# A decoder layer with 32 experts on one core: four experts instead of two in the first block, nine blocks instead of ten, and a branch two blocks later

## The chip, the core and the metric

The kernel runs on one core of a Trainium2 chip. The metric is the device time of one execution in microseconds. The kernel before took 979.65 us as the median of 3 runs (979.22 to 981.88). In the traces PE is TensorE (the matrix engine), PEld its weight loads, DVE is VectorE, ACT is ScalarE, and SP is the engine whose queue starts nearly all transfers from device memory (HBM) into the on-chip memory (SBUF). PSUM is the memory that TensorE writes its products into.

## The reference

One layer of a decoder on 256 tokens of width 2048, all in float32: an input projection, eight attention heads beside a convolution module, an output projection and a layer norm. Then comes the part that the change is about, a mixture of 32 experts:

```python
g_top = jnp.argmax(g_logits, axis=-1)              # one of 4 groups
top_p, top_i = lax.top_k(e_prob, EXPERT_TOP_K)     # 2 of the 8 experts in it
combine = (one_hot(expert_ids, N_EXPERTS) * weights[..., None]).sum(1)
h = jnp.einsum('td,edf->tef', t, w_gu)             # w_gu: 32 x 2048 x 512
act = silu(h[..., :256]) * h[..., 256:] * combine[..., None]
out = jnp.einsum('tef,efd->td', act, w_down)       # w_down: 32 x 256 x 2048
```

A second layer norm and a gated embedding (one more 2048 x 2048 product) end the layer. Each token goes to 2 of the 32 experts, so an expert has 16 tokens on average. With the inputs that the reference draws, experts 0 to 3 get 18, 2, 12 and 9 tokens; the counts of the others, in falling order, begin with 46, 43, 37, 31, 29, 29, 25.

## The kernel before

**Weights.** Each expert's weights are 6 loads of 1 MB: four pieces of `gu` (the up product, one per quarter of the 2048 inputs) and two of `dn` (the down product, one per half of the 2048 outputs). All 32 experts are read whatever the routing: 192 loads.

**Blocks.** The experts are worked off in blocks of 128 rows. A block (first rank, places) holds 2 experts with 64 places each or 4 with 32. `gather_steps` picks the tokens of a block by one-hot products (tile `xp`, line 776) and turns them into `XT` (lines 781 and 783). `block` then does the up products (`up`, tile `pg`, line 837), sums the partial results (`fold`, line 845, and `nat`, line 866), applies the activation (line 646), does the down products in two halves (`dp`, line 898), and scatters the result back into `z` (`so`, lines 910, 911 and 913). The products use TensorE in column strips: with 32 places four products stand side by side in the array, with 64 places two. The gather of the next block is woven in between the up products of the current one.

**Ranks.** The order of the experts is found at run time: `selection` sorts them by their token counts and writes the list to `order`; SP reads an expert's number from it (line 632) and loads that expert's weights. `STATIC` experts are put last in this order whatever their counts, so that they are known beforehand. They make up block 0, whose loads (`earlygu`, `earlydn`) need no routing:

```python
STATIC = 2
BLOCKS = ((30, 64), (6, 32), (10, 32), (0, 64), (14, 32), (2, 64), (18, 32), (4, 64), (22, 32), (26, 32))
early = [(("gu", e, g), gu[e, g]) for g in range(4) for e in range(STATIC)]
early += [(("dn", e, k), dn[e, k]) for k in range(2) for e in range(STATIC)]
```

**Slots.** The loads go into a ring of 1 MB slots: `ring2` (6), `ringp` (7) and later `ring3` (2), in the order that `places` yields. A load waits until its slot's last user is done, and SP's queue is worked off in order. At most 8 loads are under way, since each waits for one of eight transfer semaphores. The two `ring3` slots first hold the rows `ln0` and `ln1` that `first_affine` (lines 621 and 622 on DVE) reads, 16 steps in all. `prefetch(n)` emits the next n of the `early` loads.

**The branch.** If an expert has more tokens than places, extra blocks of 128 places would be needed. `spilled` counts such cases on DVE (line 1057), and `spill` (line 1073) branches over code for every possible case, ahead of the block numbered `SPILL_BEFORE`. Every engine takes part in this branch, SP too. The gather of the block behind it isn't woven in anywhere; it stands alone behind the branch.

**Order.** The stretch from the first norm through block 0 is written out by hand: within `in_order` PE, ACT and DVE keep the order of the code, with `next(b0)`, `next(gs0)` and `next(sel)` advancing the block, its gather and the selection. `warm(n, ...)` puts n products without use on TensorE (`W1` behind the router's products, `W2` behind the count). In the last block `embedding` adds products with `pw` (line 1095).

Of the kernel before, what the change touches and what calls it, by code (L numbers as in the profile page):

```python
# [27 lines left out]
NE = 32  # L28
# [8 lines left out]
RING = 7  # L37
# [1 line left out]
RING3 = 2  # L39


STATIC = 2

BLOCKS = ((30, 64), (6, 32), (10, 32), (0, 64), (14, 32), (2, 64), (18, 32), (4, 64), (22, 32), (26, 32))

CAPS = [64] * 6 + [32] * 24 + [64] * 2
SPILL = [(r, n) for r, c in enumerate(CAPS) for n in range(c, min(2 * 128, 2 * 256 // (r + 1) if r < 30 else 256), 128)]
SPILL_BEFORE = 5
W1 = 7
W2 = 4  # L50
WOUT = ((0, (0, 1)), (1, (0, 1)), (2, (0, 1)), (0, (2, 3)), (1, (2, 3)), (2, (2, 3)), (3, (0, 1, 2, 3)))
TAPS = 1.6
STEPS = 2.0
# [20 lines left out]
def _constants():  # L74
    cols, where = [], {}

    def put(name, a):
        full = np.zeros((P, a.shape[1]), np.float32)
        full[: a.shape[0]] = a
        where[name] = (sum(c.shape[1] for c in cols), a.shape[1])  # L80
        cols.append(full)
# [13 lines left out]
    put("kneg", np.full((P, NE), -NE))  # L95
    last = (STATIC - e).clip(0) * np.float32(1e5)
    put("kdiff", (e + last)[:, None] - (e + last)[None])
# [28 lines left out]
def tile_trunk(ctx, tc, xT, x, smalls, consts, win_m, win_v, wout, lnrows,  # L126
# [43 lines left out]
    def load(src, name, into=None):  # L170
        t = into or next(places_[0], ringp).tile([P, D], F32, tag="ring", name=name)
        nc.sync.dma_start(t, src)
        return t
# [28 lines left out]
    @contextmanager  # L202
    def in_order():
        traced = nc.cur_bb.bb.instructions
        mark = traced[-1]
        yield
        start = next(k for k in reversed(range(len(traced))) if traced[k] is mark) + 1
        prev = {}
        for i in traced[start:]:
            if i.engine in (PE.engine, ACT.engine, DVE.engine):  # L210
                if i.engine in prev:
                    tc.add_manual_dep(
                        i, prev[i.engine].name,
                        mybir.DependencyInfo(mybir.DependencyClass.NoSync, mybir.DependencyReason.DATA),
                        reason="in_order")
                prev[i.engine] = i
# [299 lines left out]
    def places():  # L516

        yield from [ring2] * RING2 + [ringp] * RING + [ring2] * RING2
        while True:
            yield from ring3 * RING3  # L520
            yield from [ringp] * RING + [ring2] * RING2

    def prefetch(n):
        for _ in range(n):
            key, src = early.pop(0)
            name = "early{}{}{}".format(*key)
            ready[key] = load(src, name, next(ahead_).tile([P, D], F32, tag="ring", name=name))

    for c, gs in WOUT:
# [20 lines left out]
        if c == 0:  # L550
# [3 lines left out]
            ahead_ = places()  # L554
            early = [(("gu", e, g), gu[e, g]) for g in range(4) for e in range(STATIC)]
            early += [(("dn", e, k), dn[e, k]) for k in range(2) for e in range(STATIC)]
            stock[:] = [2, 1, 1, 1, 1]
# [26 lines left out]
    def norm_stats(sts, pool, name):  # L584
        mv = pool.tile([P, NT, 2], F32, name=f"mv{name}")
        for t in range(NT):
            DVE.bn_aggr(mv[:, t], sts[t])
        r = pool.tile([P, NT], F32, name=f"r{name}")
        tmp = pool.tile([P, NT], F32, name=f"rt{name}")
        rstd_of(mv[:, :, 1], r, tmp, NT)  # L590
        nmr = pool.tile([P, NT], F32, name=f"nmr{name}")
        DVE.scalar_tensor_tensor(nmr, mv[:, :, 0], -1.0, r, op0=ALU.mult, op1=ALU.mult)
        return [(mv[:, t, 0:1], r[:, t:t + 1], nmr[:, t:t + 1]) for t in range(NT)]

    hTh, hTl = [], []

    prefetch(len(early))
    places_[0] = ahead_
    stM.close()
    znp = stH.enter_context(tc.tile_pool(name="znp", bufs=1, side="right"))  # L600
# [386 lines left out]
    with in_order():  # L987
        mvr = norm_stats(st1, bp, "n1")
        warm(W1, "r1")
        sel = selection()  # L990
        gs0 = gather_steps(BLOCKS[0], name(0), by=(pm, comb))
        b0 = block(BLOCKS[0], name(0), static=True)
        aff = first_affine()

        def affine_steps(n):
            for _ in range(n):
                next(aff, None)

        for c in range(NCH):
            first_norm(c)  # L1000
        next(sel)
        warm(W2, "r2")
        next(sel)
        next(gs0)
        next(sel)
        next(gs0)
        next(sel)
        next(gs0)
        next(gs0)
        next(sel)  # L1010
        next(b0)
        affine_steps(3)
        next(gs0)
        next(gs0)
        next(sel)
        next(b0)
        affine_steps(2)
        next(gs0)
        next(gs0)
        ACT.activation(dum, epsc, AF.Silu)  # L1020
        next(sel)
        next(b0)
        affine_steps(3)
        next(gs0)
        next(sel)
        next(gs0)
        next(b0)
        gs1 = gather_steps(BLOCKS[1], name(1))
        next(gs1)
        affine_steps(8)  # L1030
        stB.close()
        stC = ExitStack()
        cp = stC.enter_context(tc.tile_pool(name="cp", bufs=1))
        next(b0)
        for _ in range(2):
            next(gs1)
        next(b0)
        for _ in range(2):
            next(gs1)
        next(b0)  # L1040
        for _ in range(2):
            next(gs1)
        next(b0)
        for _ in range(3):
            next(gs1)
        next(b0)
        b1 = block(BLOCKS[1], name(1))
        for _ in range(4):
            next(b1)
        for _ in b0:  # L1050
            pass

    def spilled():

        over = sp.tile([P, len(SPILL), NT], F32, tag="over", name="over")
        for i, (r, n) in enumerate(SPILL):
            DVE.tensor_scalar(over[:, i], poss[:, :, r], float(n), None, op0=ALU.is_gt)
        many = sp.tile([P, 1 + len(SPILL)], F32, tag="many", name="many")
        DVE.tensor_reduce(many[:, 1:], over, axis=AX.X, op=ALU.add)
        DVE.tensor_reduce(many[:, 0:1], many[:, 1:], axis=AX.X, op=ALU.add)  # L1060
        total = pst([P, CH], "total", "x")
        PE.matmul(total[0:1, :1 + len(SPILL)], C("ones")[:, 0:1], many, start=True, stop=True)
        flags = rp.tile([1, 1 + len(SPILL)], I32, name="flags")
        DVE.tensor_copy(flags, total[0:1, :1 + len(SPILL)])
        return flags
# [33 lines left out]
    flags = spilled()  # L1099
    last = len(BLOCKS) - 1  # L1100
    for i, shape in enumerate(BLOCKS):
        if not i:
            continue
        if i == SPILL_BEFORE:
            spill(flags, any_)
# [5 lines left out]
        if i == last:  # L1111
            stH.close()
            gp_ = ctx.enter_context(tc.tile_pool(name="gp", bufs=1, side="right"))
            side, share, total = embedding(gp_), 5, 16
        if i == SPILL_BEFORE - 1:
            any_ = counted(flags, 0)
        coming = iter(())
        if i < last and i + 1 != SPILL_BEFORE:
            coming = gather_steps(BLOCKS[i + 1], name(i + 1))
# [208 lines left out]
```

## Time and profile before

| | |
|---|---|
| median of 3 runs | 979.65 us (979.22 to 981.88) |
| the profiled execution | 983.18 us, its span 981.3 us |
| busy: PE, PEld, DVE, ACT | 909.4, 596.4, 521.8, 356.4 us |
| moved | 294.48 MB, mean 300 GB/s |
| mean granted TensorE clock | 0.97 |

All rows below come from that one execution, in microseconds from the start of its span. Its own time is 3.5 us above the median. The stretches that matter here: the router and block 0 from 358 to 418.5, blocks 1 to 4 from 418.5 to 602.1, the branch from 602.1 to 614.6 with a gather behind it until 623, blocks 5 to 8 from 623 to 814.4, block 9 (the last) until 876.2, and from there the gate product to the end. A busy PE says little about what bounds the kernel, since PE is busy in stretches of both kinds; what a stretch moves per microsecond says more.

### The profile page before, as it was taken

What the parts mean: (1) busy time and instruction counts of PE and PEld (TensorE: products, weight loads), DVE (VectorE), ACT (ScalarE), POOL (GpSimd) and SP (SyncE); (2) the same over time, 40 slices, a digit from 0 to 9 for tenths busy, and PEclk for the clock granted to TensorE, in tenths of its full rate; (3) what the DMA queues carried; (4) which work ended last, traced back from release to release, by engine and by line L of the source; (5) the groups of instructions that cost most, each with busy time, mean ns of one, the idle gap of its engine ahead of it and who ended that gap; (6) DMA issues with size and microseconds to landing.
All of it is one profiled execution on the core that took longest, in us unless ns stands there. A gap on an engine that the chain in (4) does not pass through costs nothing. (4 is left out here: it accounts for less than half of the span.)

```text
span 981.3 us, 14211 instructions
## 1 busy us (share of the span) xinstructions
PE 909.4 (93%) x5339; PEld 596.4 (61%) x5339; DVE 521.8 (53%) x1110; ACT 356.4 (36%) x698; POOL 3.0 (0%) x14
## 2 busy tenths in 40 slices
PE   7999999999999989998989974999899988989997
PEld 7999889999878875443434311634343432247886
DVE  6989898889887455434141303123222321067875
ACT  6454455666684343212212110211111211226553
POOL 0000000000000000000000000000000000000000
PEclk9999999999999989999999978899999999999999
DMA  9868755445459348699999998988999799995721
GB/s 343 357 166 272 297 199 171 150 162 173 157 192 403 135 158 300 262 404 423 424 424 423 425 423 338 424 349 297 415 424 373 296 425 425 424 419 206 229 73 43
DMA packets 44622, 294.48 MB, mean 300 GB/s; under 512 B 5160, under 2 KB 5800, under 8 KB 10240
## 3 DMA queue, kind: packets, MB, share of 16 engines
q1 hardware_dynamic: 43568, 290.85, 75.5%
q0 software_dynamic: 976, 2.63, 1.7%
q8 instruction: 44, 0.72, 0.3%
q14 instruction: 34, 0.28, 0.1%
HBM read 289.78 MB, written 3.67 MB: 299 GB/s over the span
## 5 line engine op out<-in xcount | busy, mean ns | idle before, releaser
L837 PE MATMUL pgb<-gub,XTb 128*32 128x512 f32 (+1 forms) x960 | 149.0, 607 | 7.1 <-DMA gub<-in_gu_dram 7.0
L776 PEld LDWEIGHTS xpb<-Sb,zn 128*128 128x128 f32 x640 | 80.2, 199 | 59.3 <-issue 41.7
L357 DVE SCALAR_TENSOR_TENSOR yall<-u,sml,yall 128x256 f32<-128x256 f32 x240 | 108.6, 478 | 0.3
L776 PE MATMUL xpb<-Sb,zn 128*128 128x128 f32 x640 | 92.4, 294 | 14.6 <-PEq L1073 12.6
L783 DVE TENSOR_SCALAR XTb<-xpb,gbc 128x128 f32<-128x128 f32 x80 | 32.7, 409 | 124.4 <-ACT XTb L781 121.3
L898 PE MATMUL dpb<-dnb,aTb 128*32 128x512 f32 (+1 forms) x480 | 94.7, 612 | 1.0 <-DVE aTb L877 0.9
L781 ACT ACTIVATE XTb<-xpb,gbc 128x128 f32<-128x128 f32 x80 | 36.6, 458 | 148.2 <-PE xpb L776 148.0
L837 PEld LDWEIGHTS pgb<-gub,XTb 128*32 128x32 f32 (+1 forms) x960 | 36.2, 115 | 79.1 <-issue 57.2
L646 DVE SCALAR_TENSOR_TENSOR atb<-atb,wb,natb 128x256 f32<-128x256 f32 x10 | 4.8, 480 | 118.2 <-ACT atb L645 118.1
L913 DVE TENSOR_TENSOR z<-z,sob 128x512 f32<-128x512 f32 x76 | 49.7, 683 | 31.4 <-PE sob L911 31.3
L177 DVE TENSOR_TENSOR Ylb<-dpb,Yhb 128x512 fp32r<-128x512 f32 x40 | 26.4, 687 | 73.6 <-ACT Yhb L176 73.6
L176 ACT CAST Yhb<-dpb 128x512 fp32r<-128x512 f32 x40 | 22.3, 588 | 113.3 <-PE dpb L898 112.1
L845 ACT COPY pgsb<-pgb 128x512 f32<-128x512 f32 x32 | 18.8, 586 | 94.1 <-PE pgb L837 91.0
L898 PEld LDWEIGHTS dpb<-dnb,aTb 128*32 128x32 f32 (+1 forms) x480 | 22.3, 116 | 46.9 <-issue 40.4
L910 PE MATMUL sob<-Yhb,sctb 128*128 128x512 f32 x76 | 34.9, 487 | 15.0 <-DVE z L913 7.5
L910 PEld LDWEIGHTS sob<-Yhb,sctb 128*128 128x128 f32 x76 | 13.6, 192 | 53.3 <-issue 21.6
L911 PE MATMUL sob<-Ylb,sctb 128*128 128x512 f32 x76 | 30.6, 430 | 0.1
L866 PE MATMUL natb<-pgsb,cst 128*32 128x512 f32 (+1 forms) x64 | 20.7, 616 | 4.9 <-ACT pgsb L845 4.9
L911 PEld LDWEIGHTS sob<-Ylb,sctb 128*128 128x128 f32 x76 | 14.2, 200 | 5.9 <-DVE Ylb L177 5.6
L1095 PE MATMUL pl<-pw,pT 128*128 128x512 f32 x32 | 16.9, 652 | 0.0
L837 PE MATMUL pgb<-earlygu,XTb 128*64 128x512 f32 x64 | 16.3, 657 | 0.0
L866 PEld LDWEIGHTS natb<-pgsb,cst 128*32 128x32 f32 (+1 forms) x64 | 3.9, 116 | 17.5 <-ACT pgsb L845 13.5
(2528 smaller groups left out, 1943.1 us busy)
## 6 DMA issues: line engine op xcount, KB each, us to landing
gub<-in_gu_dram SPq DMA_DIRECT2D x120, 1024.0 KB, 18.4
dnb<-in_dn_dram SPq DMA_DIRECT2D x58, 1024.0 KB, 17.1
wo<-in_wout_dram SPq DMA_DIRECT2D x16, 1024.0 KB, 4.9
wg<-in_wgate_dram SPq DMA_DIRECT2D x16, 1024.0 KB, 5.8
wv<-in_win_v_dram SPq DMA_DIRECT2D x8, 1024.0 KB, 23.5
wk<-in_win_m_dram SPq DMA_DIRECT2D x8, 1024.0 KB, 4.8
wq<-in_win_m_dram SPq DMA_DIRECT2D x8, 1024.0 KB, 4.8
earlygu<-in_gu_dram SPq DMA_DIRECT2D x8, 1024.0 KB, 9.5
```

Of the source, the lines that this page charges most:

```text
L176: ACT.copy(h, src)
L177: return DVE.tensor_tensor(l, src, h.bitcast(F32), op=ALU.subtract)
L357: yield DVE.scalar_tensor_tensor(y, u[:, k:k + T], cw[:, c, k:k + 1], y, op0=ALU.mult, op1=ALU.add)
L776: PE.matmul(xp[:, k], zn[t][:, kt * P:(kt + 1) * P], S[:, t, :P], start=t == 0, stop=t == 1)
L781: ACT.activation(xs[:, 0], xp[:, 0], AF.Identity, bias=gbc[:, 1, kt:kt + 1], scale=gbc[:, 0, kt:kt + 1])
L783: DVE.tensor_scalar(xs[:, 1], xp[:, 1], gbc[:, 0, kt:kt + 1], gbc[:, 1, kt:kt + 1], op0=ALU.mult, op1=ALU.add)
L837: PE.matmul(pgs_[e][j * M:(j + 1) * M], XT[:, k, e * M:(e + 1) * M], gp[k], start=kt < G, stop=kt >= KT - G, tile_position=(0, j * M) if G ...
L866: PE.matmul(nat[e * M:(e + 1) * M], C(st), folds[e], start=True, stop=True, tile_position=(0, e * M))
L898: last = PE.matmul(dps[n][j * M:(j + 1) * M], aT[:, k, e * M:(e + 1) * M], dp[e][2 * k + n % 2], start=k == 0, stop=k == 1, tile_position= ...
L910: PE.matmul(o, table(n)[:, ts_], Yh[n], start=True, stop=False)
L911: PE.matmul(o, table(n)[:, ts_], Yl[n], start=False, stop=True)
L913: DVE.tensor_tensor(zs, zs, o, op=ALU.add)
```

## The change

Block 0 takes four experts with 32 places each. Of the other 28 ranks, four have 64 places and 24 have 32, in eight blocks. The branch stands ahead of block 7. The loads of block 0 become 24; 13 of them are emitted before the first norm, and 4, 4 and 3 behind the first three groups of block 0's up products. `W1` goes from 7 to 14 and `W2` from 4 to 2.

```diff
-STATIC = 2
-BLOCKS = ((30, 64), (6, 32), (10, 32), (0, 64), (14, 32), (2, 64), (18, 32), (4, 64), (22, 32), (26, 32))
-CAPS = [64] * 6 + [32] * 24 + [64] * 2
-SPILL_BEFORE = 5
-W1 = 7
-W2 = 4
+STATIC = 4
+BLOCKS = ((28, 32), (4, 32), (0, 64), (8, 32), (2, 64), (12, 32), (16, 32), (20, 32), (24, 32))
+CAPS = [64] * 4 + [32] * 28
+SPILL_BEFORE = 7
+W1 = 14
+W2 = 2
...
-    prefetch(len(early))
+    prefetch(RING)
...
         next(b0)
+        prefetch(4)
         affine_steps(3)
...
         next(b0)
+        prefetch(4)
         affine_steps(2)
...
         next(b0)
+        prefetch(3)
         affine_steps(3)
```

The list of cases behind the branch grows from 21 to 25 (`SPILL`, whose bound for the known experts now goes by `NE - STATIC`).

On SP's queue, at the end of the output projection and before block 1, this stands in the kernel before (`earlydn10` is the first half of expert 1's down weights, `gub100` the first load of block 1, and the brackets name what a row waits for):

```order
L172 DMA earlydn00_4114<-in_dn_dram 128x2048 [waits DMAHW0_49,DVE_49]
L172 DMA earlydn10_4116<-in_dn_dram 128x2048 [waits DMAHW1_49,DVE_49]
L172 DMA earlydn01_4118<-in_dn_dram 128x2048 [waits DMAHW3_49,DMAHW2_49,DVE_49]
L172 DMA earlydn11_4120<-in_dn_dram 128x2048 [waits DMAHW4_49,DVE_49]
L172 DMA ln0_4131<-in_lnrows_dram 128x2048 [waits PE_49]
L172 DMA ln1_4133<-in_lnrows_dram 128x2048 [waits DMAHW5_49]
L632 TENSOR_LOAD order_4140 [waits DVE_49]
L172 ISA
L172 DMA gub100_4554<-in_gu_dram 128x2048 [waits DMAHW6_49,DVE_49]
```

In the changed kernel the same place, from `ln1` on, reads:

```order
L172 DMA ln1_4135<-in_lnrows_dram 128x2048 [waits DMAHW6_49]
L172 DMA earlygu13_4298<-in_gu_dram 128x2048 [waits DMAHW7_49,PE_49]
L172 DMA earlygu23_4300<-in_gu_dram 128x2048 [waits DMAHW0_49,PE_49]
L172 DMA earlygu33_4302<-in_gu_dram 128x2048 [waits DMAHW1_49,PE_49]
L172 DMA earlydn00_4304<-in_dn_dram 128x2048 [waits DMAHW2_49,PE_49]
L172 DMA earlydn10_4352<-in_dn_dram 128x2048 [waits DMAHW3_49,PE_49]
L172 DMA earlydn20_4354<-in_dn_dram 128x2048 [waits DMAHW4_49,PE_49]
L172 DMA earlydn11_4401<-in_dn_dram 128x2048 [waits DMAHW5_49,PE_49]
L172 DMA earlydn30_4356<-in_dn_dram 128x2048 [waits DMAHW6_49,DVE_49]
L172 DMA earlydn01_4358<-in_dn_dram 128x2048 [waits DMAHW7_49,DVE_49]
L172 DMA earlydn21_4403<-in_dn_dram 128x2048 [waits DMAHW0_49,PE_49]
L172 DMA earlydn31_4405<-in_dn_dram 128x2048 [waits DMAHW1_49,PE_49]
```

Eleven loads of known experts now stand between `ln1` and the reading of `order`; two of them, `earlydn30` and `earlydn01`, take the `ring3` slots and wait for DVE, and everything behind them on SP waits with them.

On PE, at block 0's fourth group of up products, the kernel before has (`srt` and `wpb0` are the end of the selection and of the gather, `xpb10` the gather of block 1):

```order
L748 MATMUL srt_4362<-perm_4143,tsb_4342 128x32 x4
L794 MATMUL wpb0_4371<-cst_72,Swb0_4368 128x1 x2
L837 MATMUL pgb00_4271<-earlygu03_4110,XTb06_4333 64x512 x4
L837 MATMUL pgb01_4276<-earlygu13_4112,XTb06_4333 64x512 x4
L776 MATMUL xpb10_4403<-Sb1_4384,zn0_4126 128x128
```

and the changed kernel:

```order
L748 MATMUL srt_4417<-perm_4145,tsb_4383 128x32 x4
L794 MATMUL wpb0_4428<-cst_72,Swb0_4423 128x1 x2
L837 MATMUL pgb00_4278<-earlygu03_4122,XTb06_4374 32x512 x4
L837 MATMUL pgb01_4283<-earlygu13_4298,XTb06_4374 32x512 x4
L837 MATMUL pgb02_4288<-earlygu23_4300,XTb06_4374 32x512 x4
L837 MATMUL pgb03_4293<-earlygu33_4302,XTb06_4374 32x512 x4
L776 MATMUL xpb10_4472<-Sb1_4449,zn0_4128 128x128
```

The group has four experts of 32 places in place of two of 64; three of its four loads are among the eleven that are emitted late.

## Rows read from the trace of the kernel before

**Rows 1.** Page, part 2: GB/s moved in 40 equal slices of the span.

```profile
GB/s 343 357 166 272 297 199 171 150 162 173 157 192 403 135 158 300 262 404 423 424 424 423 425 423 338 424 349 297 415 424 373 296 425 425 424 419 206 229 73 43
```

**Rows 2.** Windows, start:end, length; busy (x count) per engine; PE clock, DMA share, GB/s.

```profile
369.70:394.00 24.30, 23.72 (x128) 12.16 (x129) 15.07 (x43) 8.22 (x19) 0.00 (x0) 0.93 0.83 303
394.00:418.50 24.50, 22.23 (x120) 12.37 (x116) 10.90 (x43) 7.51 (x16) 0.00 (x0) 0.93 0.74 277
...
467.10:512.40 45.30, 40.48 (x287) 17.13 (x286) 12.26 (x27) 9.34 (x20) 0.00 (x0) 1.00 1.01 424
512.40:557.60 45.20, 42.15 (x189) 18.75 (x188) 11.94 (x23) 7.88 (x17) 0.00 (x0) 1.00 1.01 425
557.60:602.10 44.50, 36.49 (x223) 10.10 (x222) 8.88 (x15) 5.63 (x11) 0.00 (x0) 0.88 0.92 378
602.10:623.00 20.90, 7.95 (x49) 7.67 (x49) 4.21 (x15) 2.29 (x5) 0.00 (x0) 0.67 1.01 419
...
670.20:719.00 48.80, 43.67 (x294) 18.51 (x293) 14.43 (x31) 9.23 (x20) 0.00 (x0) 0.96 0.99 393
...
814.40:876.20 61.80, 56.18 (x266) 16.80 (x266) 10.77 (x18) 13.11 (x24) 0.00 (x0) 0.95 1.02 423
```

**Rows 3.** Windows again, cut where the rate of the transfers changes.

```profile
420.00:580.00 160.00, 145.12 (x906) 58.80 (x894) 41.15 (x82) 29.01 (x61) 0.00 (x0) 0.98 1.01 423
580.00:600.00 20.00, 16.82 (x83) 5.28 (x82) 6.18 (x11) 3.28 (x7) 0.00 (x0) 0.88 0.80 322
640.00:700.00 60.00, 55.26 (x322) 24.24 (x321) 15.96 (x36) 12.60 (x27) 0.00 (x0) 1.00 0.87 338
740.00:780.00 40.00, 37.25 (x188) 17.16 (x190) 13.34 (x29) 8.34 (x18) 0.00 (x0) 1.00 0.81 320
```

**Rows 4.** Page, part 6: issues of `gu` loads, size, median us to landing.

```profile
gub<-in_gu_dram SPq DMA_DIRECT2D x120, 1024.0 KB, 18.4
```

**Rows 5.** Groups by line and form, up products of block 2, then of block 3.

```profile
L837 PE MATMUL pgb<-gub,XTb 128*32 128x512 f32 x128 | 15.5, 595 | 0.0
...
L837 PE MATMUL pgb<-gub,XTb 128*64 128x512 f32 x64 | 15.9, 602 | 0.0
```

**Rows 6.** Timeline of PE in block 0: start, us, instruction, count.

```profile
370.88 3.65 PE L837 MATMUL pgb<-earlygu,XTb 128*64 128x512 f32 x16
...
376.44 3.65 PE L837 MATMUL pgb<-earlygu,XTb 128*64 128x512 f32 x16
...
389.31 5.35 PE L837 MATMUL pgb<-earlygu,XTb 128*64 128x512 f32 x16
...
402.94 3.65 PE L898 MATMUL dpb<-earlydn,aTb 128*64 128x512 f32 x16
```

**Rows 7.** Timeline of DVE, the last two steps of the affine.

```profile
393.27 0.68 DVE L621 SCALAR_TENSOR_TENSOR z<-zn,ln 128x512 f32<-128x512 f32 x1
...
394.01 0.68 DVE L622 SCALAR_TENSOR_TENSOR z<-ln,z 128x512 f32<-128x512 f32 x1
```

**Rows 8.** Timeline of SP's queue: block 1's first loads, and around the branch.

```profile
369.68 50.30 SPq L172 DMA_DIRECT2D gub<-in_gu_dram  x16
...
559.62 16.37 SPq L172 DMA_DIRECT2D dnb<-in_dn_dram  x8
597.10 4.89 SPq L172 DMA_DIRECT2D gub<-in_gu_dram  x8
```

**Rows 9.** Timeline of PE, first instruction behind the branch.

```profile
614.61 5.94 PE L776 MATMUL xpb<-Sb,zn 128*128 128x128 f32 x32 [12.59 <-PEq L1073]
```

**Rows 10.** Timeline of PE around the warming products.

```profile
359.82 1.36 PE L242 MATMUL warmr<-cst 128*128 128x128 f32 x10
363.39 0.21 PE L697 MATMUL pos<-Aas,cbtri 128*128 128x32 bf16 x1 [2.21 <-DVE Aas L694]
...
364.10 2.08 PE L242 MATMUL warmr<-cst 128*128 128x128 f32 x8
```

**Rows 11.** Groups of PE in the last block: busy, mean ns, idle before.

```profile
L837 PE MATMUL pgb<-gub,XTb 128*32 128x512 f32 x128 | 19.0, 631 | 3.7 <-DMA gub<-in_gu_dram 3.6
```

More of the change, by code (lines that the diff above doesn't have):

```diff
@@ L39 @@
 RING3 = 2
-STATIC = 2
-BLOCKS = ((30, 64), (6, 32), (10, 32), (0, 64), (14, 32), (2, 64), (18, 32), (4, 64), (22, 32), (26, 32))
-CAPS = [64] * 6 + [32] * 24 + [64] * 2
-SPILL = [(r, n) for r, c in enumerate(CAPS) for n in range(c, min(2 * 128, 2 * 256 // (r + 1) if r < 30 else 256), 128)]
-SPILL_BEFORE = 5
-W1 = 7
-W2 = 4
+STATIC = 4
+BLOCKS = ((28, 32), (4, 32), (0, 64), (8, 32), (2, 64), (12, 32), (16, 32), (20, 32), (24, 32))
+CAPS = [64] * 4 + [32] * 28
+SPILL = [(r, n) for r, c in enumerate(CAPS) for n in range(c, min(2 * 128, 2 * 256 // (r + 1) if r < NE - STATIC else 256), 128)]
+SPILL_BEFORE = 7
+W1 = 14
+W2 = 2
 WOUT = ((0, (0, 1)), (1, (0, 1)), (2, (0, 1)), (0, (2, 3)), (1, (2, 3)), (2, (2, 3)), (3, (0, 1, 2, 3)))
```

## The prediction

> **What bounds the kernel now.** I read the rate of the transfers over the whole span first, because PE is busy nearly everywhere and so says little. From slice 18 on (24.5 us each, so from 417 us) the row stands at 423 to 425 for long stretches, with dips to 338, 349, 297, 373 and 296 [rows 1]. No stretch stays above that level, so 424 GB/s is what this chip moves when it always has something to move. One load of 1024 KB [rows 4] is 1.0486 MB and takes 1.0486 / 424 = 2.473 us; a block of four experts is 24 loads or 59.4 us, a block of two 12 loads or 29.7 us.
>
> Then I set the blocks beside it. Block 2 (32 places) takes 45.3 us and block 3 (64 places) 45.2 us, both at 424 to 425 GB/s [rows 2]. PE's time is the same for both kinds: the up products are 15.5 us for four experts in four strips and 15.9 us for two in two strips [rows 5]. So on PE a block costs about 45 us whatever its kind, while its weights cost 59.4 or 29.7 us. The expert stage is two chains of nearly equal length that lean on each other through 15 slots. Where blocks with 32 places follow each other, PE ends up waiting for weights: block 4 has 36.5 us of work in 44.5 us and a clock of 0.88 [rows 2], and the last block waits 3.6 us for `gub` [rows 11]. Where blocks with 64 places come, the slots are full and the transfers wait: 640 to 700 moves 338 GB/s, 740 to 780 moves 320 [rows 3]. Before the stage, from 369.7 to 418.5, the transfers run at 303 and 277 GB/s [rows 2], since they wait for slots.
>
> **The change part by part.**
>
> *Blocks.* The bytes stay: 192 loads. One block of two experts, 45.2 us of PE time by [rows 2], goes, and block 0 takes four experts in the time of two, since its up group of 3.65 us [rows 6] becomes 32 instructions in four strips, a fourth of the 128 that took 15.5 us [rows 5], so 3.9 us. Behind it block 0 gets four more instructions of `nat` and four of transposes on PE; at the 0.6 us of one instruction [rows 5] that is under 5 us, and about a fourth of it where four strips run side by side. I cost it at nothing: the transfers set the pace from there on, and if they didn't, it would be some 1 to 2 us. PE loses a whole block; whether the end follows depends on the transfers, so I count these.
>
> *Head start.* Before, 303 x 24.3 + 277 x 24.5 = 14.15 MB or 13.5 loads move between 369.7 and 418.5 [rows 2]; with the 12 loads of block 0 already there that is 25.5 of 192 at the start of block 1. After, 13 are there. The next seven loads (three `earlygu`, four `earlydn`) wait for slots that block 0's first two groups free. The first group runs 370.88 to 374.5, so an expert's quarter is free at about 371.8; the second ends at 380.1 [rows 6]. Seven loads take 17.3 us and are in by about 391. Then SP's queue stands at `earlydn30` until DVE has read `ln0` for the last time, at 393.27 + 0.68 = 394.0, and `ln1` 0.8 us later [rows 7]. From 394.0 on nothing holds it but the rate: 24.5 / 2.473 = 9.9 loads until 418.5. That makes 13 + 7 + 9.9 = 29.9, a lead of 4.4 loads or 10.9 us. Block 0 doesn't suffer: `earlygu13` to `earlygu33` are in by about 382 and are used from 389.3; `earlydn30` by 394 + 5 = 399 and is used from 402.9 [rows 6]. If DVE's affine came later, stream and products would slip with it one for one. The lead is at least 0 (the old rate) and at most 12.
>
> *Dips.* In 640 to 700 the shortfall is 60 x (1 - 338/424) = 12.2 us, in 740 to 780 it is 40 x (1 - 320/424) = 9.8 us [rows 3], together 22.0. After, the slots don't fill. At 45.2 us a block the stream delivers 18.3 loads: a block of two gains 6.3 loads on PE, a block of four loses 5.7. From a lead of some 6 loads at block 1 the order 32, 64, 32, 64, 32, 32 goes to about 2, 8, 2, 8, 3 and then to waiting in block 6. It never reaches 15, so all 22.0 us come back. The least I would allow is half, 11.
>
> *Branch.* SP issues block 4's last load at 576 and the next at 597.1 [rows 8]; 580 to 600 lacks 20 x (1 - 322/424) = 4.8 us [rows 3]. PE stands still 12.59 us [rows 9], and with the lone gather behind the branch 602.1 to 623 is 20.9 us [rows 2]. Ahead of block 7 the same things happen once, with the transfers just as full, so I leave both prices as they are. What PE's sequencer waits for the row doesn't say; between half the price and twice it lie 6 us less and 12 us more, and that stays in the range.
>
> *The end of the stream.* 192 loads and 2.25 for the embedding are wanted. Before: 418.5 + (194.25 - 25.5) x 2.473 + 22.0 + 4.8 = 862.6, and the last block ends at 876.2 [rows 2], 13.6 us later. After: 418.5 + (194.25 - 29.9) x 2.473 + 4.8 = 829.7, and with the same 13.6 us behind it 843.3.
>
> *PE as a check.* Block 6's last load is number 144: 418.5 + 114.1 x 2.473 = 700.7. Block 4's last load, issued at 576 [rows 8], was in by about 593 (17 to 18 us behind the issue [rows 4]), and PE left the block at 602.1 [rows 2], some 10 us later; so now it reaches the branch at 710.7. With 20.9 us for branch and gather, 48.8 us for a block of four like block 6 of before and 61.8 us for the last [rows 2] the end is 842.2. The two chains agree within 1.1 us. They hand over to each other, and after waits PE runs with a lower clock (0.88 in block 4, 0.67 around the branch [rows 2]); I add 2 us and take 845.2, that is 31 us less than 876.2.
>
> On the bandwidth the Trainium skill speaks too. Its page "DMA: Bandwidth & Descriptors", section "Where 436 GB/s comes from", gives a ceiling of 435.2 GB/s for the 16 ports. By that figure a load would take 2.409 us, the stream of the changed kernel would end near 819, and PE's chain of 842 would decide alone. The trace's fullest rows stand at 424 to 425, so I keep these.
>
> *Warming products.* Ten of them took 1.36 us, and PE idled 2.21 us behind them [rows 10]. Fourteen instructions more are about 1.9 us and fit into that gap; four instructions less behind the count save up to 1.0 us of the 2.08 us [rows 10]. A clock kept up there could give another 1.8 us at the start of the gather, and an overrun could cost 1.7. I take 0 of the range -2.8 to +1.7. The four added steps of `spilled` on DVE stand among the affine's: 0.5 us at most, inside the lead's bounds.
>
> *The sum.* Lead 10.9 and dips 22.0 give 32.9 us of stream, less 2 for the handover: 31. The span goes from 981.3 to about 950.3 and the profiled execution from 983.18 to 952.2. That execution lies 3.5 us above the median of the runs, so I set the 31 against the median: 979.65 - 31 = 948.6.
>
> **The rivals.**
>
> *The queue stands longer.* Eleven loads now precede the reading of `order`, and two wait for DVE. If DVE's affine ended not at 394 but behind the next down products, at about 406 [rows 6], or the branch cost 12 us more where the stream is full, the gain would be 31 - 12 = 19: 960.7. For it speaks that SP is strictly in order; against it that the affine stands on DVE ahead of everything that block 0 needs later.
>
> *PE decides alone.* If the transfers had reserves, the whole block would come off: 979.65 - 45.2 = 934.5. Against it: no full slice of [rows 1] exceeds 425.
>
> *The clock falls, and it ends slower.* The place is the blocks of four behind waiting weights. There the row of the block that waited shows a granted clock of 0.88 against 1.00 in those that didn't [rows 2]. Eight blocks have about 7 x 41.3 + 56.2 = 345 us of PE work and 33 us besides; between 420 and 876.2, less the branch's 20.9, lie 435 us. So it turns slower from a mean granted clock of 345 / (435 - 33) = 0.86 on; at 0.82 it is 19 us slower, 998.6. Against it: the last block waited 3.6 us and still has 0.95 [rows 2, 11], and my sum has waits only in block 6 and the last. The Trainium skill holds for it: "TensorE: Matmul & The Clock Gate", section "HAM oscillation — how this bites in real kernels", describes a kernel whose products wait for transfers again and again and start each burst on the low clock. Here that would be the blocks of four.
>
> *It isn't the same work.* With 32 places for experts 0 to 3, one with over 32 tokens would take the branch and add a block of its own, 45 us or more: 994 or above. Their counts are 18, 2, 12 and 9, and rank 4 has 29, so nothing spills.
>
> **How the numbers follow.** The forecast gets 0.82 (its own range 943 to 955: lead and branch a few us either way), the longer queue 0.10, PE alone 0.04, the clock 0.03, spilling 0.01. The range goes to 938 and 961: it leaves out PE alone, the slower cases and the worst of the longer queue. About 0.3%, 3 us, is what a measurement of this kernel can tell from no change. Faster by more: 0.82 + 0.04 + 0.08 of the longer queue = 0.94; within it 0.02; slower 0.04.
>
> **What would show it.** In the changed kernel the transfers run at 424 GB/s from about 394 to 700 without a dip, then one dip at the branch, and on to about 830. SP issues `earlydn30` near 394. Block 0 has 32-place products and starts block 1 within 2 us of 418.5. PE waits for `gub` in block 6, a few us, and in the last block. The last block ends near 845, with the 105 us behind it unchanged. I am wrong if dips remain between 420 and 690, if block 0 stalls for `earlydn`, or if the granted clock of the blocks of four lies under 0.9.

## The result and the profile after

The changed kernel takes 947.77 us as the median of 4 runs (947.23 to 949.38); the kernel before, in 4 runs beside it, takes 979.43 us (978.40 to 981.88). The ratio is 0.9676, with a 95% interval of 0.9654 to 0.9697: 31.7 us faster. The forecast was 948.6 us, 31 us less. The profiled execution of the changed kernel is the one of 947.23 us (span 945.5), so it stands close to its median, while that of the kernel before stands 3.5 us above its own. Two traces set side by side therefore show some 4 us more than the change's 31.7.

First the rate of the transfers over the whole span, the page's row in 40 slices (23.6 us each here), against [rows 1]:

```profile
GB/s 334 368 179 242 325 203 188 140 174 152 160 179 329 264 184 271 332 420 423 424 420 423 422 421 422 421 421 424 421 316 418 420 420 422 417 418 209 217 78 33
```

From the 18th slice on (402 us) the row stands at 417 to 424 until the expert stage ends, with a single dip, 316, at the branch. Before there were five. Next come the stretches of the changed kernel, cut at the blocks (start:end, length; busy and count of PE, PEld, DVE, ACT, POOL; granted clock, DMA share, GB/s): block 0 in two parts, blocks 1, 2, 3 and 6, branch and gather, block 7, the last block, the rest.

```profile
363.50:388.50 25.00, 24.32 (x195) 13.49 (x197) 15.62 (x45) 8.88 (x22) 0.00 (x0) 0.93 0.72 295
388.50:412.00 23.50, 21.11 (x166) 11.95 (x162) 10.97 (x46) 8.28 (x18) 0.00 (x0) 1.00 0.96 392
412.00:472.20 60.20, 49.20 (x301) 19.38 (x300) 16.92 (x36) 9.34 (x20) 0.00 (x0) 0.91 1.01 422
472.20:517.40 45.20, 42.15 (x189) 18.76 (x188) 12.66 (x27) 7.89 (x17) 0.00 (x0) 1.00 1.01 422
517.40:563.30 45.90, 41.09 (x291) 17.66 (x290) 13.14 (x29) 9.24 (x20) 0.00 (x0) 1.00 1.01 421
...
655.00:707.00 52.00, 37.16 (x219) 8.91 (x218) 7.54 (x13) 5.62 (x11) 0.00 (x0) 0.92 0.91 373
707.00:723.50 16.50, 8.79 (x44) 8.01 (x44) 5.22 (x17) 1.83 (x4) 0.00 (x0) 0.69 1.01 420
723.50:774.50 51.00, 46.14 (x318) 20.86 (x316) 12.83 (x26) 11.33 (x25) 0.00 (x0) 1.00 1.01 420
774.50:840.10 65.60, 55.16 (x266) 16.52 (x266) 10.80 (x18) 13.14 (x24) 0.00 (x0) 0.95 1.02 418
840.10:945.50 105.40, 98.89 (x453) 78.96 (x451) 77.19 (x138) 54.63 (x98) 0.00 (x0) 0.99 0.45 164
```

The two kernels can be set against each other on one axis. These windows are of the kernel before; the second set, behind it, is of the changed kernel with the same cuts.

```profile
340.00:363.50 23.50, 20.39 (x107) 16.65 (x106) 15.09 (x47) 10.49 (x18) 0.00 (x0) 0.99 0.50 180
363.50:412.00 48.50, 45.97 (x261) 28.00 (x262) 26.00 (x90) 16.36 (x36) 0.00 (x0) 0.89 0.73 272
412.00:418.50 6.50, 6.18 (x22) 2.20 (x18) 1.74 (x3) 1.17 (x2) 0.00 (x0) 0.83 0.43 147
418.50:840.00 421.50, 371.94 (x2137) 154.59 (x2136) 107.55 (x221) 74.56 (x158) 0.00 (x0) 0.96 0.96 396
```

```profile
340.00:363.50 23.50, 21.95 (x135) 18.57 (x134) 15.11 (x52) 11.33 (x18) 0.00 (x0) 1.00 0.60 219
363.50:412.00 48.50, 45.42 (x357) 25.44 (x359) 26.60 (x90) 17.16 (x39) 0.00 (x0) 0.96 0.84 342
412.00:418.50 6.50, 6.10 (x42) 2.28 (x42) 3.85 (x8) 0.59 (x1) 0.00 (x0) 1.00 1.02 423
418.50:840.00 421.50, 357.33 (x2058) 144.46 (x2057) 100.34 (x207) 74.82 (x157) 0.00 (x0) 0.96 1.00 415
```

Up to 418.5 the first three rows give 180 x 23.5 + 272 x 48.5 + 147 x 6.5 = 18.4 MB before and 24.5 MB after: 6.1 MB or 5.8 loads more, 14.4 us of stream at 424 GB/s. From there to 840 the rate is 415 in place of 396 GB/s: 19 x 421.5 = 8.0 MB, 7.6 loads, 18.9 us. Together that is 33 us of stream. The last block ends at 840.06 in place of 876.2 [rows 2], and what follows it takes 105.4 us, 105.1 before. Of these 36.1 us, 2.6 arise ahead of block 0: the warming products `warmr` behind the router start at 357.22, not 359.82 [rows 10]. The change does nothing there; in the eight traces of kernels that have it this start lies between 357.22 and 360.07, so the 2.6 us are spread among executions.

Where PE waits for weights in the changed kernel, from the view of its waits (line, releaser: us in total, times, longest) and its timeline in block 1, the branch and the last block:

```profile
PE pgb L837 <- DMA gub<-in_gu_dram: 22.1, 15, 6.4
...
PE xpb L776 <- DVE Sb L766: 7.6, 1, 7.6
...
PE dpb L898 <- DMA dnb<-in_dn_dram: 2.6, 2, 2.1
```

```profile
411.94 3.64 PE L837 MATMUL pgb<-gub,XTb 128*32 128x512 f32 x32
...
434.42 1.07 PE L837 MATMUL pgb<-gub,XTb 128*32 128x512 f32 x8 [1.43 <-DMA gub<-in_gu_dram]
436.90 1.06 PE L837 MATMUL pgb<-gub,XTb 128*32 128x512 f32 x8 [0.57 <-DMA gub<-in_gu_dram]
439.38 1.07 PE L837 MATMUL pgb<-gub,XTb 128*32 128x512 f32 x8 [1.42 <-DMA gub<-in_gu_dram]
...
715.94 7.67 PE L776 MATMUL xpb<-Sb,zn 128*128 128x128 f32 x40 [7.60 <-DVE Sb L766]
...
786.22 1.94 PE L837 MATMUL pgb<-gub,XTb 128*32 128x512 f32 x8 [6.36 <-DMA gub<-in_gu_dram]
```

In block 1 PE takes eight products of 1.07 us, then waits up to 1.4 us, so that one load of 2.49 us follows the other: PE follows the stream. The waits stand in blocks 1, 6 and the last, 24.7 us in all.

SP's queue in the changed kernel, the counterpart of [rows 8]:

```profile
366.32 2.04 SPq L172 DMA_DIRECT2D earlygu<-in_gu_dram  x3
368.89 21.82 SPq L172 DMA_DIRECT2D earlydn<-in_dn_dram  x8
391.52 30.81 SPq L172 DMA_DIRECT2D gub<-in_gu_dram  x16
...
664.02 17.72 SPq L172 DMA_DIRECT2D dnb<-in_dn_dram  x8
703.43 30.87 SPq L172 DMA_DIRECT2D gub<-in_gu_dram  x16
```

At the branch SP issues nothing for 703.43 - 681.74 = 21.7 us; before it was 597.1 - 576.0 = 21.1.

### The profile page after: what moved, and what is told of

Read it like the earlier page. It is cut to its first block, busy times and chain, and to the rows that moved or that the text cites. A ratio compares the mean times of both kernels' runs of the same rounds, so it can differ in the third digit from the quotient of the medians.

```text
span 945.5 us, 13989 instructions
## 1 busy us (share of the span) xinstructions
PE 862.3 (91%) x5263; PEld 575.2 (61%) x5263; DVE 509.1 (54%) x1090; ACT 349.5 (37%) x684; POOL 3.0 (0%) x14
## 5 line engine op out<-in xcount | busy, mean ns | idle before, releaser
L837 PE MATMUL pgb<-gub,XTb 128*32 128x512 f32 (+1 forms) x896 | 135.6, 621 | 22.2 <-DMA gub<-in_gu_dram 22.1
L776 PEld LDWEIGHTS xpb<-Sb,zn 128*128 128x128 f32 x576 | 71.7, 199 | 45.7 <-issue 28.7
L776 PE MATMUL xpb<-Sb,zn 128*128 128x128 f32 x576 | 81.7, 292 | 8.4 <-DVE Sb L766 7.6
L837 PEld LDWEIGHTS pgb<-gub,XTb 128*32 128x32 f32 (+1 forms) x896 | 31.6, 115 | 93.2 <-issue 50.6
L898 PE MATMUL dpb<-dnb,aTb 128*32 128x512 f32 (+1 forms) x448 | 82.6, 603 | 3.3 <-DMA dnb<-in_dn_dram 2.6
L177 DVE TENSOR_TENSOR Ylb<-dpb,Yhb 128x512 fp32r<-128x512 f32 x36 | 23.5, 687 | 70.8 <-ACT Yhb L176 70.8
L913 DVE TENSOR_TENSOR z<-z,sob 128x512 f32<-128x512 f32 x68 | 44.5, 684 | 19.3 <-PE sob L911 19.2
L910 PE MATMUL sob<-Yhb,sctb 128*128 128x512 f32 x68 | 29.6, 467 | 17.3 <-DVE z L913 9.3
L911 PE MATMUL sob<-Ylb,sctb 128*128 128x512 f32 x68 | 26.6, 423 | 0.0
L837 PE MATMUL pgb<-earlygu,XTb 128*32 128x512 f32 x128 | 16.5, 651 | 0.0
L1099 ACT COPY ple<-pl 128x512 f32<-128x512 f32 x8 | 4.7, 586 | 28.5 <-PE pl L1098 28.5
## 6 DMA issues: line engine op xcount, KB each, us to landing
wv<-in_win_v_dram SPq DMA_DIRECT2D x8, 1024.0 KB, 23.5
```

The costliest lines, as they stand in the source:

```text
L776: PE.matmul(xp[:, k], zn[t][:, kt * P:(kt + 1) * P], S[:, t, :P], start=t == 0, stop=t == 1)
L837: PE.matmul(pgs_[e][j * M:(j + 1) * M], XT[:, k, e * M:(e + 1) * M], gp[k], start=kt < G, stop=kt >= KT - G, tile_position=(0, j * M) if G ...
L898: last = PE.matmul(dps[n][j * M:(j + 1) * M], aT[:, k, e * M:(e + 1) * M], dp[e][2 * k + n % 2], start=k == 0, stop=k == 1, tile_position= ...
L910: PE.matmul(o, table(n)[:, ts_], Yh[n], start=True, stop=False)
L911: PE.matmul(o, table(n)[:, ts_], Yl[n], start=False, stop=True)
L913: DVE.tensor_tensor(zs, zs, o, op=ALU.add)
```

## The experiments

All times are medians. Ratios are to the kernel before as measured beside each run. The kernel before that stood beside e11 and e12 took 973.62 us in its one run, less than any other run of it, so the times of these two say nothing; only their traces are used.

| run | based on | us | ratio (95%) |
|---|---|---|---|
| the change | | 947.77 | 0.9676 (0.9654 to 0.9697) |
| e3_fewer_bytes | after | 909.46 | 0.9287 (0.9250 to 0.9323) |
| e4_less_pe | after | 947.13 | 0.9677 (0.9649 to 0.9706) |
| e5_no_hold | after | 943.58 | 0.9644 (0.9616 to 0.9672) |
| e6_order | after | 970.79 | 0.9926 (0.9896 to 0.9956) |
| e1_warm_old | after | 952.49 | 0.9723 (0.9700 to 0.9745) |
| e2_branch5 | after | 948.15 | 0.9674 (0.9651 to 0.9696) |
| e7_block0_alone | after | 950.16 | 0.9694 (0.9671 to 0.9718) |
| e8_before_warm | before | 969.02 | 0.9903 (0.9867 to 0.9940) |
| e9_before_w1 | before | 968.30 | 0.9883 (0.9851 to 0.9916) |
| e10_before_w2 | before | 975.22 | 0.9955 (0.9932 to 0.9978) |
| e11_before_w2_1 | before | 975.63, one run | |
| e12_before_w2_3 | before | 980.77, one run | |

**Do the transfers or PE set the end?** The theory is the forecast's: the stream of loads does. The rival is that PE's lost block alone made the gain. One run, e3, takes bytes away (it leaves out the second half of the down weights of blocks 1 to 7), the other, e4, takes away PE's work.

```diff
+                    elif hf and not static and not done:
+                        dp[e] = first_half[e]
...
-                        dp[e] = weights_of("dn", e, hf)
+                        dp[e] = first_half[e] = weights_of("dn", e, hf)
```

> The changed kernel, but in blocks 1 to 7 the second half of each expert's down weights isn't loaded: the products of that half read the first half again, so the result is not the reference's. 24 of the 192 loads go, 24 x 2.488 = 60 us of stream, no product goes. Theory (the stream of weights sets the pace behind block 0): the stream chain drops out, PE's own chain decides, that is seven blocks at 45 to 48 us, the branch, and the last block without its waits: the last block ends near 808 instead of 840, 30 to 34 us earlier, about 915 us. Rival (PE decides alone already): nothing changes, 948 us.

```diff
-PE.matmul(o, table(n)[:, ts_], Yh[n], start=True, stop=False)
-PE.matmul(o, table(n)[:, ts_], Yl[n], start=False, stop=True)
+PE.matmul(o, table(n)[:, ts_], Yh[n], start=True, stop=True)
```

> The changed kernel without the second product of each scatter (the low parts Yl at line 911), except in the closing half of the last block, so the result loses precision. PE loses 8 x 0.42 = 3.4 us in a block, 27 us in all; no load goes. Theory (stream): only what lies behind the last loads counts, 1 to 4 us faster, 944 to 947 us. Rival (PE decides alone): 25 to 27 us faster, about 922 us.

Fewer bytes gave 38 us, less work on PE 0.6 us, inside the interval. PE's busy time fell by 10.3 us (862.3 to 852.0) and not by 27, at a granted clock of 0.94 in place of 0.96 from 418.5 to 840, and even these 10 us don't show in the time. With less work PE only waits longer (its waits in e4_less_pe, against 22.1 and 2.6):

```profile
PE pgb L837 <- DMA gub<-in_gu_dram: 24.6, 20, 7.0
...
PE dpb L898 <- DMA dnb<-in_dn_dram: 3.7, 3, 2.0
```

The 60 us of stream that e3 takes away don't all come back. Its row of the page shows where they stay: the dips return (322, 314, 333, 363, 299), as they stood in the kernel before. PE also stands 13.0 us at the branch in e3, not 7.6.

```profile
GB/s 338 377 173 229 314 225 188 162 166 158 154 172 197 420 144 226 318 341 423 421 423 422 369 424 421 322 314 423 419 333 363 299 423 408 412 421 174 224 65 35
```

**Does the order of the blocks matter, as the slot argument says?** Here all blocks of 32 places but the last come first.

```diff
-BLOCKS = ((28, 32), (4, 32), (0, 64), (8, 32), (2, 64), (12, 32), (16, 32), (20, 32), (24, 32))
+BLOCKS = ((28, 32), (4, 32), (8, 32), (12, 32), (16, 32), (20, 32), (0, 64), (2, 64), (24, 32))
```

> The changed kernel with the blocks in another order: 28 (known), 4, 8, 12, 16, 20 with 32 places, then 0 and 2 with 64, then 24. The same blocks, bytes and products. Theory: blocks of four in a row make PE wait (13.9 us each in blocks 2 to 5), and two blocks of two behind the branch then find the slots full, so the stream idles: some 24 us slower, 965 to 975 us. Rival (the dips of the kernel before came from its two blocks more with 64 places and not from their places in the order): 948 us.

970.79: 23 us of the gain are gone with the same bytes and the same products. The lead is used up early, and PE waits 35.5 us for `gub`. Then the blocks of 64 places fill the slots: the stretch from 770 to 800 moves 114 GB/s, which lacks 30 x (1 - 114/424) = 21.9 us.

```profile
PE pgb L837 <- DMA gub<-in_gu_dram: 35.5, 34, 1.7
```

```profile
770.00:800.00 30.00, 28.44 (x147) 14.01 (x146) 5.68 (x13) 6.70 (x15) 0.00 (x0) 1.00 0.31 114
```

**What does SP's standing at `earlydn30` cost?** The late loads of known experts go to slots that PE frees, none to a `ring3` slot, so that SP doesn't wait for the affine.

```diff
-        yield from [ring2] * RING2 + [ringp] * RING + [ring2] * RING2
+        yield from ([ring2] * RING2 + [ringp] * RING) * 2 + [ring2] * RING2
```

> The changed kernel with another order of slots: the late loads of block 0 take slots of the ring that block 0's first groups free, and the two slots that wait for DVE's affine come into the order only behind them. SP's queue then never stands at earlydn30. Between 363 and 388.5 the stream ran at 295 GB/s of 422, which is 7.5 us short. Theory (stream): 5 to 7 us of this come back and the end moves by as much: 941 to 943 us. Rival (the head start isn't worth its time, since PE's chain is as long): 0 to 2 us, 946 to 948 us.

943.58 (942.77 to 945.12 in 6 runs): 4.2 us less than the change by the medians, 3.1 us by the ratios; no run of one lies among those of the other, though the intervals of the ratios overlap. In its queue block 1's loads begin at 382.02 and not at 391.52, and PE waits 17.3 us for `gub`:

```profile
370.02 11.19 SPq L172 DMA_DIRECT2D earlydn<-in_dn_dram  x8
382.02 37.51 SPq L172 DMA_DIRECT2D gub<-in_gu_dram  x16
```

So the hold is real; its price, 3 to 4 us, lies between the two theories (5 to 7 and 0 to 2) and in neither. This version is the fastest found, 35 us below the kernel before.

**What are the branch's place and the warming products worth?**

```diff
-SPILL_BEFORE = 7
+SPILL_BEFORE = 5
```

> The changed kernel with the branch ahead of block 5 instead of block 7. Theory (stream): SP stands still for about 21 us once wherever the branch is, the stream loses 4 to 6 us once, and PE's standstill is hidden behind waits for weights later: within 2 us of 947.8. Rival (the place of the branch is worth time of its own, since PE's standstill of some 16 to 21 us with the lone gather lands on the chain): 5 us or more in either direction.

```diff
-W1 = 14
-W2 = 2
+W1 = 7
+W2 = 4
```

> The changed kernel with the old numbers of warming products (7 and 4). In the trace of the changed kernel the first gather ran in 3.1 us instead of 4.9 and block 0 began 8.7 us behind the router's second product group instead of 11.9. Theory (the warming products keep the clock up, DVE's affine ends earlier, and the stream with it): 2 to 3.5 us slower, 950 to 951 us. Rival (my forecast's term, 0): within 1 us of 947.8.

e7_block0_alone has both edits, so that only the blocks and the late loads are left of the change.

> The main part alone: four known experts with 32 places in block 0, nine blocks and the late loads, but the old warming products (7 and 4) and the branch ahead of block 5. Theory: all of the gain but the 2 to 3.5 us of the warming products, 950 to 951 us. Rival (the branch's place carries a part): 955 us or more.

The branch's place is worth nothing (0.9674 and 0.9676); SP's gap there is 21.8 us. Without the new warming products the changed kernel is 4.7 us slower, and its interval doesn't meet the change's; between e7 and e2, with the branch ahead of block 5, it is 2.0 us, with intervals that overlap. Blocks and late loads put alone on the kernel before give 29.2 us, against 31.7 for the whole change.

The traces of the kernels with this order of blocks and all the bytes bear out the stream: e1, e2, e4, e5, e7 and the change all move 415 GB/s from 418.5 to 840. They differ in what moves from 340 to 418.5: 288 and 291 GB/s with the old warming products (e7, e1), 298 to 312 with the new (e2, e4, the change), 329 in e5, the fastest.

Then the warming products alone, on the kernel before (`W1 = 14`, `W2 = 2`):

> The kernel before with only the new numbers of warming products (14 and 2). Theory: block 0 begins 3 us earlier there too, and since block 0's known weights are loaded by then and PE is on the chain behind it, the end comes 1 to 3.5 us earlier, 976 to 978.5 us. Rival (it helps only where the stream's start hangs on it): 979.4 within 1 us.

A miss: it is 10.4 us faster, three times the theory's most. PE's timeline shows two causes. In the changed kernel, as in this run, the stretch from the router's warming products to block 0 reads (here of the changed kernel, against [rows 10]):

```profile
357.22 2.92 PE L242 MATMUL warmr<-cst 128*128 128x128 f32 x24
360.79 0.19 PE L697 MATMUL pos<-Aas,cbtri 128*128 128x32 bf16 x1 [0.64 <-DVE Aas L694]
...
361.41 0.71 PE L242 MATMUL warmr<-cst 128*128 128x128 f32 x4
361.96 1.06 PE L776 MATMUL xpb<-Sb,zn 128*128 128x128 f32 x8
363.09 2.08 PE L776 MATMUL xpb<-Sb,zn 128*128 128x128 f32 x16
365.10 3.77 PE L837 MATMUL pgb<-earlygu,XTb 128*32 128x512 f32 x32
```

The 14 added instructions fill the gap and delay nothing: `pos` starts 3.57 us behind the start of `warmr` in both. The gather behind runs on the upper level of the clock, 2.4 GHz (granted clock 1.00 from 357.2 to 365.1; 0.60 from 365.9 to 370.9 before): 8 products in 1.06 us, which took 1.91 before, and 16 in 2.08 against 2.94. From `pos` to the first up product it is 4.3 us in place of 7.5. In e8 block 0 starts 3.1 us earlier as well (367.82). The other cause lies at the branch: PE stands still 6.75 us there and not 12.59. Two questions followed: is it `W1` or `W2`, and why does the standstill change? Two runs change one of the numbers each.

```diff
-W1 = 7
+W1 = 14
```

> The kernel before with W1 = 14 alone (W2 stays at 4): 14 more warming instructions ahead of the count, none taken away behind it. With W1 = 14 and W2 = 2 together the kernel before came to 969.0 instead of 979.4, and PE's standstill at the branch fell from 12.6 us to about 6.8. Theory, the clock through the selection does it: block 0 then starts about 2 us earlier (3 us less about 1 us of products that stay behind the count), the standstill at the branch is about 7 us or 12.6 as may be, and the time is 970 to 974. Rival, the standstill depends on how many instructions lie ahead of the branch on PE: with 14 more instead of 10 more it may be of either size, and the time follows it: about 970 with a short one, about 977 with a long one, block 0 starting 2 us earlier in both.

```diff
-W2 = 4
+W2 = 2
```

> The kernel before with W2 = 2 alone (W1 stays at 7): 4 warming instructions less behind the count. Theory, the clock through the selection does it and W2 only takes away its own time: block 0 starts within 1 us of 370.9, the standstill of PE at the branch stays near 12.6 us, and the time is 977 to 980. Rival, the standstill depends on the place of the branch in PE's instructions: then 4 instructions less could shorten it to about 7 us without any change at the selection, and the time would be 972 to 975.

`W1` alone gives the whole gain (968.30), with 7.2 us of standing at the branch. `W2` alone gives 4.4 us, near the rival's 972 to 975 but without its shorter standstill; with it block 0 starts 2.5 us earlier (368.35), 0.9 us of that from ahead of the router, and at the branch something new stands: 3 products, then a pause. Two kernels, `W2 = 1` and `W2 = 3`, test whether the pause moves with the number of instructions.

> The kernel before with W2 = 1: 6 warming instructions less behind the count, all ahead of the branch on PE. With 4 less, PE ran 3 products behind the branch, then idled 4.49 us with nothing that the profile names, where the kernel before idled 12.59 us in one piece; with 10 or 14 more, the 4.5 us were gone. Theory, PE pauses some 4.5 us at a fixed place of its instructions: then 2 less again let 5 products run ahead of a pause of 4 to 5 us. Rival, the pause has another cause: it stands behind 3 products again, or is gone, or is of another length.

> The kernel before with W2 = 3: 2 warming instructions less behind the count. Theory, a pause at a fixed place of PE's instructions: 1 product runs ahead of a pause of 4 to 5 us. Rival: 3 products, or none and 12.6 us in one piece as in the kernel before, or no pause.

PE's first instructions behind the branch, with 2 (e12), 4 (e10) and 6 (e11) warming instructions less ahead of it:

```profile
609.68 0.55 PE L776 MATMUL xpb<-Sb,zn 128*128 128x128 f32 x1 [7.25 <-DVE Sb L766]
614.69 6.17 PE L776 MATMUL xpb<-Sb,zn 128*128 128x128 f32 x31 [4.46 <-issue]
```

```profile
603.72 0.98 PE L776 MATMUL xpb<-Sb,zn 128*128 128x128 f32 x3 [7.69 <-DVE Sb L766]
609.18 5.52 PE L776 MATMUL xpb<-Sb,zn 128*128 128x128 f32 x29 [4.49 <-issue]
```

```profile
606.52 1.40 PE L776 MATMUL xpb<-Sb,zn 128*128 128x128 f32 x5 [7.22 <-DVE Sb L766]
611.39 8.12 PE L776 MATMUL xpb<-Sb,zn 128*128 128x128 f32 x43 [3.47 <-issue]
```

1, 3 and 5 products run ahead of the pause, which lasts 4.5, 4.5 and 3.5 us: it stands at a fixed place of PE's instructions. By this series the place lies just ahead of the first product in the kernel before, so that some 7.3 us of waiting for DVE and a pause of 5.3 add up to the 12.59 of [rows 9]. With 10 or 14 instructions more (e8, e9) no such pause is seen there, nor in the changed kernel (7.60). It isn't gone from every kernel with the change: in e3 PE's first product starts at 693.81, 6.1 us behind DVE's first instruction (687.72), and nothing is named for which it waits. The Trainium skill, "Runtime: NRT & Kernel Launch", section "Instruction fetch mechanics", says that instructions are fetched in blocks of fixed length and that a taken branch out of the blocks at hand must wait for a fetch. A pause that keeps its place in the code agrees with that; that it is this fetch no row shows.

How do the 10.4 us of e8 divide? e10 is the counterpart, since it has the earlier start and still the pause. Here are the kernel before, e10 and e8, from block 0's first up product to block 1's:

```profile
370.90:418.50 47.60, 44.75 (x237) 23.45 (x236) 25.66 (x84) 15.27 (x34) 0.00 (x0) 0.93 0.79 296
```

```profile
368.40:412.60 44.20, 41.35 (x237) 22.64 (x236) 25.53 (x83) 15.28 (x34) 0.00 (x0) 1.00 0.86 318
```

```profile
367.80:413.80 46.00, 43.15 (x239) 23.10 (x238) 25.63 (x84) 15.26 (x34) 0.00 (x0) 0.96 0.83 307
```

In e10 block 0 also is 3.4 us shorter. In the kernel before two groups of 16 products take 5.35 us in it, at 389.31 [rows 6] and at 410.48, where e10's take 3.65: the granted clock in them is 0.68 and 0.67 against 1.00. Behind block 0 e10 and e8 differ (first e10, then e8):

```profile
418.50:840.00 421.50, 371.95 (x2123) 154.69 (x2123) 104.33 (x215) 75.16 (x159) 0.00 (x0) 0.96 0.96 396
```

```profile
418.50:840.00 421.50, 374.89 (x2156) 155.60 (x2156) 105.16 (x217) 76.81 (x162) 0.00 (x0) 0.98 0.98 405
```

With the pause the rate is 396 GB/s (e10), 397 (e12) and 399 (e11), and 396 in the kernel before; without it, 405 (e8, e9). So the earlier start and the faster block 0 are worth about the 4.4 us of e10, and the missing pause about the 6 to 7 us between e10 and e8 or e9. Each trace is one execution, so this division is rough, and whether the clock in block 0 follows from the warming products isn't shown (e8 has 0.96).

This bears on the change. The 29.2 us and the 10.4 don't add up to 31.7. One thing that both contain is the missing pause: in e7 PE stands still 7.0 us, in e8 6.75. With the same warming products in both kernels, blocks, late loads and the branch's place are worth 969.02 - 947.77 = 21 us. Whether the changed kernel would pay for the pause at its branch no run tests.

## Why the prediction was right

**The bound** (right). The stream sets the end of the changed kernel: e3 and e4 show it. The rival "PE decides alone" falls by e4.

**Head start** (right). 10.9 us of lead at 418.5 were forecast, with nothing for the warming products. With the old ones, e7 and e1 move 288 and 291 GB/s from 340 to 418.5 against 234 (18.4 MB in 78.5 us), which is 10.0 and 10.6 us of stream. The whole change has 14.4. `earlydn30` was to be held to 394.0 and the stream free from there on. The affine's last reads of the two rows end at 388.6 and 389.4, and block 1's first product starts at 411.94 and not "within 2 us of 418.5": the whole stretch came earlier, by 2.6 us ahead of the warming products and 3.2 us behind them. The hold itself is as described, and block 0 doesn't wait for `earlydn`.

**Dips** (right in size, the cause in part). 22.0 us were to return and none to remain but the branch's; 18.9 were measured. What lacks is the rate: 421 to 422 GB/s and 418 to 420 later, not 424, some 3 us over the stage. e6 shows that the return hangs on the order of blocks, as the count of loads said. But the forecast put all of the dips down to the blocks of 64 places. e8 has the old blocks and no pause at the branch, and moves 405 GB/s where the kernel before moves 396: 9 x 421.5 = 3.8 MB, 8.9 us of stream. So about half of what came back can be had without another order of blocks; the forecast had no such term.

**Waits** (partly wrong). They were to come "in block 6, a few us, and in the last block". Block 1 waits too, takes 60.2 us and not 45, and has a clock of 0.91. The count went by whole blocks, from "a lead of some 6 loads". But a block takes 16 of its 24 loads for the up products, in its first half, and there the lead is gone at once. It cost the stream nothing (422 GB/s): 24 loads at 2.485 us are 59.6 us, so block 1 went at the stream's pace.

**Warming products** (wrong). "I take 0 of the range -2.8 to +1.7": 2.0 to 4.7 us of gain were measured on the changed kernel. The four products left out gave 1.4 us (0.71 in place of 2.08), for which the bound had 1.0, and the gather 1.7 (0.85 and 0.86), for which it had 1.8. The bound was sound, and taking 0 of it was the error: the earlier end of the affine carried the gain on to the transfers. This and the 2.6 us that are spread among executions are the likely rest of the lead; no run parts them.

**Branch** (right in place, half wrong in price). SP's 21.7 us and the one dip stayed: in 680 to 720 the transfers move 358 GB/s, which lacks 6.2 us where 4.8 were taken. PE's 12.59 us fell to 7.60. The forecast took the 12.59 for the branch's price, but some 5 us of it were the pause, which moves with a few instructions and isn't seen in the changed kernel. With the gather it was 708.4 to 723.5, 15.1 us in place of 20.9. That the pause is missing there is luck for the forecast, which left "6 us less and 12 us more" in its range.

**PE's check** (right by offsetting errors). The arrival at the branch, forecast for 710.7, was at 708.4; branch and gather took 5.8 us less, block 7 2.2 more (51.0) and the last 3.8 more (65.6, with 8.3 us of waits for `gub`). The forecast 842.2 stands against 840.1.

**The clock** (rival, didn't come). PE's clock fell to 0.91 and 0.92 in blocks 1 and 6, which wait, and was 1.00 in blocks 2, 3 and 7. The mean from 418.5 to 840 was 0.96, above the forecast's point of 0.86. In block 1, behind the waits of up to 1.4 us, it was 0.74 from 440 to 460 us. The Trainium skill, "TensorE: Matmul & The Clock Gate", section "HAM oscillation — how this bites in real kernels", describes products that wait for transfers again and again and start each burst on the low clock. Block 1 shows that in a mild form.

**The sum** (right in part by luck): 14.4 + 18.9 = 33.3 us of stream against 32.9. Two terms are off by 3 us each, in opposite directions. The last block's end came 36.1 us earlier in the traces where 31 were forecast. The time agrees, 31.7 against 31, because the trace of the kernel before lies 3.5 us above its median and that of the changed kernel 0.5 below its own. And the measured 31.7 hold things that the forecast didn't have: the warming products' gain and, as e8 suggests, the missing pause.

## What to carry to other kernels

Where loads and products have the same length in sum, count the loads that are in at each block's start, in the order the block uses them: blocks that eat loads and blocks that free them must alternate, and a lead is spent in a block's first half. A load that waits for a slot with a slow user holds all that stand behind it on its queue, so give late loads the slots that come free first. Before a standstill at a branch is taken as its price, move the code by a few instructions and measure again. And price a change with the small gains in both kernels: here 29.2 us became 21 once the kernel before had the new warming products too.

## What the runs showed of the hardware

Behind a branch TensorE paused 3.5 to 4.5 us behind 1, 3 and 5 products with 2, 4 and 6 instructions less ahead of it, that is at a fixed place of its instructions (one trace each); with 10 and 14 more no pause was seen. SP's time without an issue at the branch (21.1 us before, 21.3 in e8, 21.7 after, 18.1 in e3) didn't go with it. Warming products through a gap of 2.2 us kept the clock's upper level and made the 24 products behind it 1.7 us shorter. A group of 16 products took 5.35 us at a granted clock of 0.68 and 3.65 at 1.00. Behind five waits of 0.6 to 1.4 us between products of 1.07 us (block 1 after, from 431.9 on) the granted clock was 0.74 from 440 to 460 us. Loads of 1 MB issued back to back ran at 420 to 424 GB/s for 280 us without a dip.
